# A transformer stack on one core: the two heads of a pair given to the scheduler ahead of the next pair's projections

## The chip, the cores and the metric

The kernel runs on one core of a Trainium2 chip. The metric is the device time of one execution, in microseconds, as the median of several runs. Three runs of the kernel before took 1758.92, 1760.01 and 1761.11 us; the median is 1760.01 us.

## The reference, cut to what matters

The input x has 512 positions of 1024 channels, in float32. Four attention layers come first: MLA, sliding window (SWA), forget-gate attention (FOX), MLA. A second block follows (four mixers, a SwiGLU feed-forward, a gated embedding), which the change doesn't touch. Each of the four layers has 16 heads, and its shape is the same:

```python
h = x @ w_in                                   # queries, keys, values, gate (MLA: through low ranks)
s = q @ k.T * scale (+ per-head bias), causal   # per head; SWA: a window of 128 keys
o = softmax(s) @ v                              # per head, 512 x 64
y = (o * silu(gate)) @ w_out
x = layernorm(8 ** 0.25 * x + y)
```

## The kernel before, in words

**Precision.** Every large product is made from high and low parts in fp32r: `mm3` (L155 to L159) issues three matmuls for one product of 128 contraction rows. A weight block is loaded by SyncE (`w`, L135), its high part is cast on ScalarE (L138) and its low part is subtracted on GpSimd (L139).

**One attention layer.** Heads go two by two, as eight pairs. `pairs` (L586) is the loop over them, and MLA, SWA and FOX hand it three things:

- `prep(p)`: the projections of pair p. They write the `acc` banks of PSUM, and ScalarE and VectorE copy them out into high and low tiles. SWA: one query projection of 24 matmuls of 512 columns, and for pairs 0 and 4 a key projection (L655). FOX: a query and a key projection of 24 matmuls each (L723), for every second pair the values of the group, and for each head a bias tile (a DMA of a row broadcast, and four additions on GpSimd, L737 and L738). MLA: small projections from the low ranks, for every second pair values of the group, and three kinds of DMA that place parts of queries and keys (L520, L187).
- `head(d, p, e)`: `attend` (L390). Scores on TensorE into the two `s` banks, the bias and the row maximum on VectorE (L403), exponentials on ScalarE (L419), the division on VectorE (L427), transposes on TensorE into the two `t` banks (L443), the split of the transposed block on ScalarE and VectorE (L184, L185), and the product with the values into the one `o` bank (L452). The scores of a head live in a tile `p`, of which there are two. In these layers a head issues no DMA and nothing on GpSimd.
- `gate(p)` (L601): a projection of 24 matmuls of 512 columns, tanh on ScalarE (L605) and one operation on VectorE (L606).

`join` (L458) copies a head's output out of the `o` bank (L462 on ScalarE, L463 on VectorE) and `gated` (L465) multiplies with the gate. The output projection (`out_proj`, L283, through `layer_end`) follows: 192 matmuls of 512 columns, of which 21 of every chain of 24 don't need the last pair.

**What sets the order.** The kernel does not write out the order of an engine's queue. The program is given to the framework's scheduler (L1133), which plays it through with its own estimates of time and so lays down the order of each engine's instructions and which buffer each tile gets. Instructions that depend on one another keep their order; among those that are ready, the place in the given program ranks them. An instruction that is not ready is passed over, so a later piece of the program can run earlier. On the chip each queue is then fixed.

In the loop of `pairs` the given order is: the projections of pair p+1 (L593), the two heads of pair p (L594 and L595), the gate of pair p (L597), the gating (L598). FOX takes the pairs in the order 6, 7, 0, 1, 2, 3, 4, 5 (L749), the others from 0 to 7.

Of the kernel before, what the change touches and what calls it, by code (L numbers as in the profile page):

```python
# [88 lines left out]
class Kern:  # L89
# [496 lines left out]
    def pairs(s, order, prep, head, Wg, g0, xT, oT):  # L586

        order = list(order)
        u = {order[0]: s.gate(order[0], Wg, g0, xT)}
        d = prep(order[0])  # L590
        for p, after in zip(order, order[1:] + [None]):
            og = s.t("f", [P, S], name="og")
            nd = prep(after) if after is not None else None  # L593
            for e in range(2):  # L594
                s.join(og, e, head(d, p, e))  # L595
            if p not in u:
                u[p] = s.gate(p, Wg, g0, xT)  # L597
            s.gated(p, og, u[p], oT, after is None)  # L598
            d = nd
# [537 lines left out]
```

## Time and profile before

| | |
|---|---|
| runs shown | 1758.92, 1760.01, 1761.11 us; median 1760.01 us |
| profiled execution, its own time | 1762.84 us |
| span of the profiled execution | 1761.1 us |
| mean granted TensorE clock | 0.979 |
| busy: PE, PEld, VectorE, ScalarE, GpSimd | 96%, 81%, 55%, 50%, 49% |
| the pair loops in the span | MLA about 72 to 257 us, SWA 308 to 480, FOX 547 to 783, MLA 868 to 1046 |

TensorE is busy nearly everywhere, so the share of busy time alone doesn't show where time can be won. The table of stretches is read with two columns together: the busy time of TensorE against the length of the stretch, and the granted clock.

### The profile page before, as it was taken

The page shows a single profiled execution, that of the slowest core. Times are in us where ns is not written, and L with a number is a line of the kernel's source. Part 1 is how long each engine was busy: PE and PEld are TensorE (multiplying, and loading weights), DVE is VectorE, ACT ScalarE, POOL GpSimd, SP SyncE. Part 2 cuts the span into 40 slices and gives each one's busy share as a digit, 9 for nine tenths or more (in the row PEclk, how much of TensorE's full clock was granted, in tenths as well). Part 3 has the DMA queues.
Part 4 walks back from the last instruction along what each step waited for, and adds up shares of the span by engine and source line. Part 5 has one row for each costly group of instructions (what it writes and reads, how often), then busy time and mean ns, then how long its engine had stood idle before and what let it go on. Part 6 is the DMA issues. An engine that isn't in the chain of part 4 may idle for free.

```text
span 1761.1 us, 25691 instructions
## 1 busy us (share of the span) xinstructions
PE 1684.8 (96%) x8818; PEld 1435.2 (81%) x8818; DVE 962.0 (55%) x2223; ACT 873.8 (50%) x2054; POOL 854.4 (49%) x775
## 2 busy tenths in 40 slices
PE   8999999999999999999999998999999999999999
PEld 7888878887788888778888877877778888888877
DVE  4587654677654665766587665599544222210053
ACT  4576543666445655633576642755544333332351
POOL 1644534444255665616644523745644444443571
PEclk9999999999999999999999998999999999999999
DMA  5434534322032333314444523332332333332332
GB/s 169 132 98 114 165 104 124 99 70 87 26 97 81 101 88 93 116 51 127 120 110 103 176 61 74 91 81 64 114 90 83 98 96 96 96 100 80 105 99 72
DMA packets 190339, 173.91 MB, mean 99 GB/s; under 512 B 14280, under 2 KB 154952, under 8 KB 190208
## 3 DMA queue, kind: packets, MB, share of 16 engines
q1 hardware_dynamic: 190208, 172.27, 33.9%
q8 instruction: 70, 1.15, 0.3%
q14 instruction: 61, 0.50, 0.1%
HBM read 150.94 MB, written 6.87 MB: 90 GB/s over the span
## 4 chain that ended last, share of the span: by engine, by line
PE 52%; DVE 9%; ACT 2%; issue 2%; POOL 2%; DMA 1%; SPq 0%; ACTq 0%; POOLq 0%; DVEq 0%
PE ps_acc L157 11%; PE ps_acc L158 11%; PE ps_acc L159 11%; PE ps_s L158 4%; PE ps_s L157 4%; PE ps_s L159 4%; PE ps_o L452 2%; PE ps_t L443 2%; DVE p L427 1%; DVE sel L926 1%; ACT p L419 1%; DVE m L925 1%; DVE p L403 1%; PE ps_s L238 1%; DVE ptl L185 1%
## 5 line engine op out<-in xcount | busy, mean ns | idle before, releaser
L139 POOL TENSOR_TENSOR wl<-wr,wh 128x512 fp32r<-128x512 f32 (+2 forms) x362 | 472.7, 1316 | 421.5 <-ACT wh L138 408.7
L138 ACT CAST wh<-wr 128x512 fp32r<-128x512 f32 (+2 forms) x368 | 223.6, 613 | 364.9 <-PE ps_acc L158 125.1
L157 PE MATMUL ps_acc<-act,wh 128*128 128x512 f32 (+1 forms) x880 | 331.5, 377 | 0.9 <-DVE v L620 0.8
L158 PE MATMUL ps_acc<-act,wh 128*128 128x512 f32 (+1 forms) x880 | 330.2, 375 | 0.3 <-DVE act L185 0.2
L159 PE MATMUL ps_acc<-act,wl 128*128 128x512 f32 (+1 forms) x880 | 330.1, 375 | 0.0
L157 PEld LDWEIGHTS ps_acc<-act,wh 128*128 128x128 f32 x880 | 165.6, 188 | 27.9 <-PE ps_acc L159 1.2
L159 PEld LDWEIGHTS ps_acc<-act,wl 128*128 128x128 f32 x880 | 165.3, 188 | 27.5
L158 PEld LDWEIGHTS ps_acc<-act,wh 128*128 128x128 f32 x880 | 165.4, 188 | 27.0 <-DVE act L185 0.7
L419 ACT ACTIVATE p<-p,st 128x256 f32<-128x256 f32 (+3 forms) x288 | 153.5, 537 | 32.8 <-DVE st L410 17.3
L157 PE MATMUL ps_acc<-wh,act 128*128 128x256 f32 (+3 forms) x384 | 134.5, 350 | 7.7 <-ACT act L469 3.1
L185 DVE TENSOR_TENSOR ptl<-ps_t,pth 128x512 fp32r<-128x512 f32 (+1 forms) x200 | 117.6, 597 | 38.5 <-ACT pth L184 37.7
L184 ACT CAST pth<-ps_t 128x512 fp32r<-128x512 f32 (+1 forms) x200 | 100.3, 516 | 72.5 <-PE ps_t L443 63.0
L443 PE MATMUL ps_t<-c_ident,p 128*128 128x128 f32 x672 | 116.9, 283 | 17.3 <-DVE p L427 12.4
L427 DVE TENSOR_SCALAR p<-p,st 128x256 f32<-128x256 f32 (+3 forms) x264 | 132.1, 559 | 1.8
L159 PE MATMUL ps_acc<-wh,act 128*128 128x256 f32 (+3 forms) x384 | 130.7, 341 | 0.1
L158 PE MATMUL ps_acc<-wl,act 128*128 128x256 f32 (+3 forms) x384 | 130.4, 340 | 0.0
L443 PEld LDWEIGHTS ps_t<-c_ident,p 128*128 128x128 f32 x672 | 82.0, 143 | 33.7 <-DVE p L427 13.2
L452 PE MATMUL ps_o<-pth,v 128*128 128x256 f32 (+3 forms) x288 | 90.1, 318 | 6.3 <-DVE og L463 4.4
L452 PE MATMUL ps_o<-ptl,v 128*128 128x256 f32 (+3 forms) x288 | 88.2, 335 | 4.3 <-DVE ptl L185 4.2
L157 PEld LDWEIGHTS ps_acc<-wh,act 128*128 128x128 f32 x384 | 77.8, 203 | 16.0 <-ACT act L469 3.3
L158 PEld LDWEIGHTS ps_acc<-wl,act 128*128 128x128 f32 x384 | 77.7, 202 | 5.1 <-issue 0.5
L159 PEld LDWEIGHTS ps_acc<-wh,act 128*128 128x128 f32 x384 | 77.1, 201 | 5.5 <-DVE act L185 0.3
(371 smaller groups left out, 3801.3 us busy)
## 6 DMA issues: line engine op xcount, KB each, us to landing
wr<-in_w_gate_up_dram SPq DMA_DIRECT2D x88, 256.0 KB, 2.8
wr<-in_fox_w_in_dram SPq DMA_DIRECT2D x60, 256.0 KB, 3.1
wr<-in_w_in_dram SPq DMA_DIRECT2D x48, 256.0 KB, 2.9
wr<-in_w_down_dram SPq DMA_DIRECT2D x44, 256.0 KB, 2.6
wr<-in_swa_w_in_dram SPq DMA_DIRECT2D x40, 256.0 KB, 2.9
wr<-in_mla_w_in_dram SPq DMA_DIRECT2D x32, 256.0 KB, 3.1
qk<-qk SPq DMA_DIRECT2D x32, 256.0 KB, 3.1
wr<-in_mla_w_out_dram SPq DMA_DIRECT2D x32, 256.0 KB, 3.5
```

The lines of the kernel that those rows point to most:

```text
L138: nc.scalar.copy(h, raw)
L139: (nc.vector if dve else nc.gpsimd).tensor_sub(l, raw, h.bitcast(F32))
L157: mm(out, lh, rh, start=first, stop=False)
L158: mm(out, lh, rl, start=False, stop=False)
L159: return mm(out, ll, rh, start=False, stop=last)
L184: s.nc.scalar.copy(hi, src)
L185: s.nc.vector.tensor_sub(lo, src, hi.bitcast(F32))
L238: mm(out, q[:, e, c], kd[:, kk], start=True, stop=False)
L419: nc.scalar.activation(a, a, AF.Exp, bias=st[:, 1, i:i + 1], scale=scale, accum_out=st[:, 2, i:i + 1])
L427: nc.vector.tensor_scalar_mul(a, a, st[:, 3, i:i + 1])
L443: nc.tensor.transpose(ps[:, n:n + P], sc[:, c:c + P], s.ident)
L452: nc.tensor.matmul(o[:, j * P:j * P + m], vj, pp[:, c:c + m], start=first, stop=k == 1 and grp[-1] == max(2, grp[-1]) and j == grp[-1], sk ...
```

## The change

The call of `prep` for the next pair moves from ahead of the two heads to behind them. What is computed stays the same, and no instruction is added or removed.

```diff
         for p, after in zip(order, order[1:] + [None]):
             og = s.t("f", [P, S], name="og")
-            nd = prep(after) if after is not None else None
             for e in range(2):
                 s.join(og, e, head(d, p, e))
+            nd = prep(after) if after is not None else None
             if p not in u:
                 u[p] = s.gate(p, Wg, g0, xT)
             s.gated(p, og, u[p], oT, after is None)
```

## Rows read from the trace of the kernel before

**Rows 1.** The page's first part: the span, and busy time, share of the span and instructions of each engine.

```profile
span 1761.1 us, 25691 instructions
PE 1684.8 (96%) x8818; PEld 1435.2 (81%) x8818; DVE 962.0 (55%) x2223; ACT 873.8 (50%) x2054; POOL 854.4 (49%) x775
```

**Rows 2.** Busy time by stretch: the stretch, its length, then busy time and count of PE, PEld, DVE, ACT, POOL, the granted clock, the DMA share, GB/s. Each pair loop is cut in its body and its end; the last row is a stretch of the feed-forward.

```profile
72.00:204.00 132.00, 129.07 (x717) 111.02 (x717) 94.87 (x271) 86.04 (x238) 61.15 (x59) 0.99 0.48 129
204.00:257.00 53.00, 46.46 (x224) 37.66 (x223) 34.18 (x77) 28.16 (x64) 24.30 (x19) 0.94 0.40 124
308.00:428.00 120.00, 115.29 (x620) 98.18 (x619) 87.64 (x244) 78.99 (x203) 52.81 (x41) 0.99 0.28 84
428.00:480.00 52.00, 46.54 (x226) 37.69 (x225) 36.15 (x93) 27.36 (x73) 13.57 (x12) 0.90 0.14 44
547.00:742.00 195.00, 191.36 (x1082) 167.02 (x1081) 121.74 (x310) 118.35 (x282) 113.25 (x116) 0.98 0.34 95
742.00:783.00 41.00, 35.73 (x167) 29.07 (x167) 27.20 (x60) 21.57 (x53) 14.24 (x12) 0.92 0.23 67
868.00:1001.00 133.00, 129.01 (x723) 110.44 (x721) 99.12 (x278) 87.29 (x240) 62.66 (x59) 1.00 0.48 131
1001.00:1046.00 45.00, 41.86 (x209) 34.73 (x209) 26.02 (x67) 23.22 (x55) 12.08 (x9) 0.96 0.28 86
1408.00:1452.00 44.00, 44.00 (x195) 36.44 (x195) 9.44 (x12) 14.43 (x24) 21.18 (x17) 1.00 0.34 99
```

**Rows 3.** The timeline of PE at the end of FOX's loop: start, length, engine, line, tiles. The first row is the last matmul of the last gate, the second the first of the output projection.

```profile
741.83 0.39 PE L159 MATMUL ps_acc<-act,wl 128*128 128x512 f32 x1
742.06 0.39 PE L157 MATMUL ps_acc<-wh,act 128*128 128x512 f32 x1
```

**Rows 4.** The timeline of VectorE from 742 to 778 us, its joins alone: one row ends one head of FOX.

```profile
751.72 0.68 DVE L463 TENSOR_TENSOR og<-ps_o,og 64x512 f32<-64x512 f32 x1
760.82 0.69 DVE L463 TENSOR_TENSOR og<-ps_o,og 64x512 f32<-64x512 f32 x1
769.32 0.68 DVE L463 TENSOR_TENSOR og<-ps_o,og 64x512 f32<-64x512 f32 x1 [0.47 <-ACT og L462]
776.24 0.69 DVE L463 TENSOR_TENSOR og<-ps_o,og 64x512 f32<-64x512 f32 x1
```

**Rows 5.** The group of PE's instructions from 742 to 783 us with the longest wait: busy time, mean ns of one, then the idle time before them and what ended it.

```profile
L157 PE MATMUL ps_acc<-wh,act 128*128 128x512 f32 x12 | 5.1, 421 | 3.1 <-ACT act L469 3.1
```

**Rows 6.** The timeline of PE around the scores of the first head of FOX's pair 3: the two matmuls of one score block (L238, L239), and the rows next to them.

```profile
690.15 0.22 PE L238 MATMUL ps_s<-qk 128*128 128x128 f32 x1
690.21 0.46 PE L157 MATMUL ps_acc<-act,wh 128*128 128x512 f32 x1
...
703.07 0.39 PE L159 MATMUL ps_acc<-act,wl 128*128 128x512 f32 x1
703.30 0.22 PE L239 MATMUL ps_s<-kl,qk 128*128 128x128 f32 x1
```

**Rows 7.** The groups of PE instructions between those two, from 690.25 to 703.28 us: the projections among them.

```profile
L157 PE MATMUL ps_acc<-act,wh 128*128 128x512 f32 x16 | 6.4, 401 | 0.0
L158 PE MATMUL ps_acc<-act,wh 128*128 128x512 f32 x16 | 6.4, 399 | 0.0
L159 PE MATMUL ps_acc<-act,wl 128*128 128x512 f32 x16 | 6.3, 392 | 0.0
```

**Rows 8.** The timeline of VectorE: the last copy of a pair's projections out of PSUM (L185, L204, L228), and L403, the first operation of a head on its scores. In order of time: MLA pair 3's first head, MLA pair 4's key, MLA pair 4's first head; SWA pair 7's query, SWA pair 6's first head, SWA pair 7's first head; FOX pair 1's key and first head; FOX pair 3's first head, its block after the wait of rows 6, FOX pair 4's key and first head.

```profile
122.24 0.68 DVE L403 CUSTOM_DVE_ANT_0 p<-ps_s,c_mask 128x512 f32<-128x512 f32 x1
...
134.04 0.68 DVE L185 TENSOR_TENSOR qk<-ps_acc,qk 128x512 fp32r<-128x512 f32 x1
...
146.84 0.68 DVE L403 CUSTOM_DVE_ANT_0 p<-ps_s,c_mask 128x512 f32<-128x512 f32 x1
...
421.08 0.69 DVE L204 TENSOR_TENSOR qk<-ps_acc,qk 64x512 fp32r<-64x512 f32 x1
...
426.77 0.28 DVE L403 CUSTOM_DVE_ANT_0 p<-ps_s,win 128x128 f32<-128x128 f32 x1
...
447.35 0.28 DVE L403 CUSTOM_DVE_ANT_0 p<-ps_s,win 128x128 f32<-128x128 f32 x1
...
616.50 0.69 DVE L228 TENSOR_TENSOR kl<-ps_acc,qk 64x512 fp32r<-64x512 f32 x1
...
625.05 0.68 DVE L403 CUSTOM_DVE_ANT_0 p<-ps_s,rope 128x512 f32<-128x512 f32 x1
...
686.86 0.68 DVE L403 CUSTOM_DVE_ANT_0 p<-ps_s,rope 128x512 f32<-128x512 f32 x1
...
703.56 0.29 DVE L403 CUSTOM_DVE_ANT_0 p<-ps_s,b 128x128 f32<-128x128 f32 x1 [3.89 <-PE ps_s L239]
...
710.01 0.69 DVE L228 TENSOR_TENSOR kl<-ps_acc,qk 64x512 fp32r<-64x512 f32 x1
...
724.48 0.69 DVE L403 CUSTOM_DVE_ANT_0 p<-ps_s,rope 128x512 f32<-128x512 f32 x1 [0.95 <-issue]
```

**Rows 9.** The timeline of PE: the scores of FOX pair 3's first head, and the last transposes of the head two before it.

```profile
681.80 0.40 PE L239 MATMUL ps_s<-kl,qk 128*128 128x512 f32 x1
...
686.65 0.62 PE L443 MATMUL ps_t<-c_ident,p 128*128 128x128 f32 x4
```

**Rows 10.** The waits of SyncE's queue, the longest: who waited for whom, us in total, times, the longest.

```profile
SPq L135 <- POOL wl L139: 755.1, 309, 19.7
```

## The prediction

> **What bounds the kernel now.** I read the page first: TensorE is busy 96% of a span of 1761.1 us, the next engine, VectorE, 55% [rows 1]. The kernel is bound by TensorE, so a change of order can only win back time in which TensorE stands idle or runs at a lower granted clock, or lose more of it. Next I cut the span by stage. A stretch of the feed-forward shows what full speed is: 44.00 of 44.00 us busy, clock 1.00, 195 matmuls of 512 columns, that is 0.2256 us for each [rows 2]. Against that stand the four pair loops. I add, for each stretch, the idle time of PE and the time lost to the clock (one minus the granted clock, times the length). The ends of the loops lose 6.5 + 3.2 = 9.7 us (first MLA, 204 to 257), 5.5 + 5.2 = 10.7 (SWA, 428 to 480), 5.3 + 3.3 = 8.6 (FOX, 742 to 783) and 3.1 + 1.8 = 4.9 (second MLA, 1001 to 1046), 33.9 us together; the bodies lose 4.2, 5.9, 7.5 and 4.0 us [rows 2]. The rest of the kernel isn't touched. So 34 us at the ends are the most that I look for, and the question is what makes them.
>
> The timeline answers it for FOX. The last gate's last matmul starts at 741.83 us and the output projection at 742.06 [rows 3], but four heads end after that, at 751.72, 760.82, 769.32 and 776.24 plus 0.69 us [rows 4]: 8.2 us from one to the next. Projections have run ahead and heads have fallen behind, so at the end there is little for TensorE besides the chains of single heads. Is it the order of this change that holds the heads back? The score block of 128 columns of FOX pair 3's first head says yes: its first matmul starts at 690.15, its second, which needs only tiles that an earlier block of the same head had used at 681.80, at 703.30 [rows 6, 9]. Between them lie 48 matmuls of 512 columns [rows 7]. That is twice 24, the query and the key of the next pair in FOX's order, pair 4: its key is copied out at 710.01 [rows 8]. VectorE stood idle 3.89 us for that second matmul [rows 8]. In the given order those 48 stand ahead of these heads; the change puts them behind.
>
> **The change part by part.** Nothing is added or removed; `prep` of the next pair loses its rank over the two heads. It changes the order only where both are ready at once.
>
> *FOX.* There they are: pair 3's heads begin at 686.86 and pair 4's key is copied out at 710.01 [rows 8]. What goes: a wait of up to 13.15 us in one head (703.30 minus 690.15) [rows 6]. What is late next: the head's tile `p`. The first operation of pair 3's first head, on scores ready after 681.80, runs at 686.86, right behind the last transposes of the head two before it, at 686.65 [rows 8, 9]; so part of any gain is spent waiting for one of two tiles. I take that heads come out one spacing, 8.2 us, earlier relative to the projections, less than the 13.15. A head's own TensorE work is 6400 columns (2560 of scores, 1280 of transposes, 2560 of the product), at 0.2256 us for 512 columns 2.8 us. Today's end, from 742 to the last join at 776.9, is 34.9 us long and has 4 x 2.8 + 19.0 = 30.2 us to fill it (19.0: four chains of 21 matmuls of the output projection that don't need the last pair); 4.7 us remain, near the 5.3 idle [rows 2]. With three heads left it is 26.7 us against 8.4 + 19.0 = 27.4: no gap. But the last join, its gating and casts are then still awaited, and the wait for them is 3.1 us [rows 5]. So of 8.6 us I count 8.6 - 3.1 = 5.5 as won. Bounds: 8.6 above; below see the second rival.
>
> *MLA, twice.* Mostly the next projections are finished long before the pair begins, but where a group's values are due they overlap: pair 3's heads begin at 122.24, pair 4's key is copied out at 134.04 [rows 8]. The body loses 4.2 and 4.0 us in all, and this is one of two such places in each [rows 2]. Between 0 and 4 I take 0.75 each, near the lower end, because a TensorE that stalls there is also short of projections, which now come later.
>
> *SWA.* Pair 7's query is copied out at 421.08, before pair 6's first head begins at 426.77 [rows 8]. Where the projections are through before the heads are ready, rank decides nothing: 0, upper bound the 10.7 us of its end.
>
> *The queues moved past.* Every DMA of `prep` (weights, FOX's rows, MLA's placing, SWA's window) sits in SyncE's queue, and FOX's bias additions in GpSimd's. A head puts nothing in either, so the order within both queues stays except against the gate's, which it already preceded and still does. SyncE mostly waits for free weight tiles (755.1 us) [rows 10]; a projection that runs later frees them later. I cost that at nothing, covered by the distance from copy-out to need: 14.5 us for FOX's pair 4 (724.48 minus 710.01), 12.8 for MLA's pair 4 (146.84 minus 134.04), 26.3 for SWA's pair 7 (447.35 minus 421.08), and least, 8.6, for FOX's pair 1 (625.05 minus 616.50) [rows 8]. Two heads of FOX put 5.6 us of TensorE work ahead of the projections, less than each of these.
>
> *Interleaving.* More changes between projections and small matmuls of heads come in. The most finely mixed stretch, the second MLA's body, runs at a clock of 1.00; the clock falls at the ends, where PE waits (0.90 and 0.92) [rows 2]. So I cost the mixing at nothing. [...]
>
> *Sum.* 5.5 + 2 x 0.75 = 7.0 us. Against the profiled execution's own 1762.84 us that is 1755.8. The median of the runs is 2.8 us below that execution, so for the median I say 1760.0 - 7.0 = **1753.0 us**.
>
> **The rivals.**
>
> *No change.* The heads are slow because only two `p` tiles exist, not because of rank. For it: rows 9, and SWA, whose end loses most though its projections run more than a pair ahead [rows 2, 8]. Against it: the 13.15 us of rows 6. Then the time is 1760, give or take the reshuffle of a few places, within 3.5. [...]
>
> *Slower: the next pair starves.* If the scheduler pushes `prep` not by 5.6 us of TensorE work but behind both heads' whole chains, 2 x 8.2 = 16.4 us, the distances above are used up: by 7.8 us at FOX's pair 1, 1.9 at its pair 4, 3.6 at MLA's pair 4. Heads would start late, and what they lose appears at the loop's end, where nothing covers it. With FOX's 7.8 alone it gives 1768; with MLA's twice, 1775. It decides from the point where the copy-out of `prep` comes more than 8.6 us later against its pair. For it: MLA's and FOX's distances are short. Against it: TensorE has gaps in every chain, and whatever is ready fills them.
>
> *All ends close.* If the lag of heads goes in all four loops, up to 33.9 us are won: 1726. Against it: SWA's 421.08 and 426.77.
>
> **How the numbers follow.** A measurement of this kernel can tell about 0.2%, 3.5 us, from no change. My forecast (3.5 to 14 us faster): 0.42. More than 14 faster: 0.08. No change: 0.28. Slower: 0.22. So faster 0.50, same 0.28, slower 0.22. The order is laid down anew for four loops, and rows show only some of the places that move, so the range goes to 1738 (two thirds of the large case's way) and to 1768 (the second rival's first price); I leave out 0.07 below and 0.10 above. The likeliest case alone spans 1746 to 1756.5.
>
> **What would show it.** Right: in FOX no head's score block split by 48 matmuls, three heads or fewer ending after the last gate, PE busier and the clock above 0.92 at that end; SWA's end much as before. Wrong: distances from copy-out to first operation of a head below zero slack with PE idle in a loop's body; or the same four heads left over at an unchanged end. The prediction as a whole fails if loops that I cost at nothing, SWA above all, move by more than FOX does.

## The result and the profile after

The change makes the kernel slower: 1781.2 us (median of 1786.51, 1782.02, 1778.68 and 1780.39) against 1759.5 us in the same session, ratio 1.013, 95% interval 1.0102 to 1.0157, or 18 to 28 us lost. The forecast was 1753.0 us, its range ended at 1768. The profiled execution after took 1786.51 us of its own, the longest of these four.

The page's engine line of the kernel after, in answer to [rows 1]:

```profile
span 1784.7 us, 25695 instructions
PE 1701.3 (95%) x8818; PEld 1443.8 (81%) x8818; DVE 963.3 (54%) x2223; ACT 878.7 (49%) x2054; POOL 852.7 (48%) x775
```

The work is the same, 8818 matmuls. To see in which layer the time went, take the end of the last transpose of each layer's output (L248) as a milestone, in both profiles; between two milestones lies one layer:

| layer | before, us | after, us | difference |
|---|---|---|---|
| load of x | 13.9 | 15.2 | +1.3 |
| MLA | 273.7 | 282.7 | +9.1 |
| SWA | 224.6 | 226.9 | +2.3 |
| FOX | 308.4 | 301.6 | -6.7 |
| MLA, second | 263.9 | 281.8 | +17.9 |
| all behind | 676.6 | 676.4 | -0.2 |

FOX gained 6.7 us in this profile, where 5.5 was forecast. The two MLA layers, forecast at 0.75 us of gain each, lost 27. The busy time by stretch of the kernel after, in the columns of [rows 2] (MLA's body and end, FOX's, the second MLA's):

```profile
72.00:204.00 132.00, 122.62 (x649) 103.93 (x648) 90.03 (x262) 83.16 (x226) 55.14 (x54) 0.95 0.41 106
204.00:268.00 64.00, 59.96 (x295) 48.99 (x294) 38.47 (x89) 32.85 (x76) 30.34 (x24) 0.97 0.50 150
555.00:747.00 192.00, 191.04 (x1102) 167.39 (x1101) 126.24 (x315) 120.66 (x290) 117.08 (x120) 1.00 0.35 98
747.00:789.00 42.00, 37.00 (x167) 29.81 (x166) 25.73 (x55) 20.23 (x46) 14.80 (x11) 0.88 0.28 80
873.00:1005.00 132.00, 121.50 (x628) 102.02 (x627) 89.37 (x260) 80.07 (x220) 52.08 (x52) 0.92 0.37 94
1005.00:1070.00 65.00, 62.33 (x311) 50.43 (x308) 38.92 (x87) 32.48 (x76) 23.79 (x18) 1.00 0.48 139
```

Add idle time of PE and time lost to the clock, as the prediction did. MLA's body loses 9.4 + 6.6 = 16.0 us where it lost 4.2, the second MLA's body 10.5 + 10.6 = 21.1 where it lost 4.0. Their ends lose less than before (6.0 and 2.7 against 9.7 and 4.9). FOX's body loses 1.0 in place of 7.5.

So the question is what holds up PE in MLA's body. The forecast had looked at pair 4's key copied out to its first head [rows 8]; here is that pair after, on VectorE:

```profile
146.97 0.68 DVE L185 TENSOR_TENSOR qk<-ps_acc,qk 128x512 fp32r<-128x512 f32 x1
...
156.90 0.69 DVE L403 CUSTOM_DVE_ANT_0 p<-ps_s,c_mask 128x512 f32<-128x512 f32 x1 [2.39 <-PE ps_s L159]
```

The copy-out came 12.9 us later than before (134.04), the head 10.1 us later (146.84). Who waits? SyncE's own queue, from 100 to 225 us, has one wait that the kernel before does not have in its list; columns: engine and line, what it waited for, total us, times, longest:

```profile
SPq L477 <- POOL qr L762: 18.3, 2, 14.1
```

and its timeline shows the hole of 17 us between two DMAs that place queries:

```profile
124.61 0.50 SPq L477 DMA_DIRECT2D qk<-qk  x1
141.64 1.15 SPq L477 DMA_DIRECT2D qk<-qr  x2
```

`qr` L762 is the last step of `rope` (L752), the rotation of the next group's queries. Its two steps on VectorE, L757 and L758, one right behind the other (134.12 and 134.73 us after), empty the acc bank that its matmuls wrote. Timelines of PE (last matmul of that projection), ScalarE (first copy of a join, L462; a gate's tanh, L605) and VectorE (L757), first of the kernel before:

```profile
98.27 0.39 PE L159 MATMUL ps_acc<-cq,wl 128*128 128x512 f32 x1
...
110.84 0.58 ACT L462 COPY og<-ps_o 64x512 f32<-64x512 f32 x1 [0.34 <-PE ps_o L452]
111.45 0.60 ACT L605 ACTIVATE f<-ps_acc 128x512 f32<-128x512 f32 x1
...
111.55 0.69 DVE L757 TENSOR_TENSOR f<-ps_acc,cos 128x512 f32<-128x512 f32 x1
```

and then of the kernel after:

```profile
104.17 0.39 PE L159 MATMUL ps_acc<-cq,wl 128*128 128x512 f32 x1
...
116.89 0.58 ACT L462 COPY og<-ps_o 64x512 f32<-64x512 f32 x1 [0.41 <-PE ps_o L452]
117.50 0.60 ACT L605 ACTIVATE f<-ps_acc 128x512 f32<-128x512 f32 x1
...
134.12 0.68 DVE L757 TENSOR_TENSOR f<-ps_acc,cos 128x512 f32<-128x512 f32 x1
...
135.85 0.58 ACT L462 COPY og<-ps_o 64x512 f32<-64x512 f32 x1
136.46 0.60 ACT L605 ACTIVATE f<-ps_acc 128x512 f32<-128x512 f32 x1
```

Before, the rotation runs 12.9 us behind its matmuls, beside the first join of pair 1. After, it runs 29.6 us behind them, beside the first join of pair 2. All that time it holds one of three acc banks. VectorE is 68% busy in this body, so it was free to run the rotation long before.

**The theory** (the rope theory below, after the name of the rotation's routine). The rotation needs two tiles named `f`, of which there are four. So does each pair: its output `og`, first written by its first join, and its gate's `u`. If the slots of one tile name are given out in the order in which the program first writes its tiles, the line before is og1, u1, a, b, og2, u2 (a and b are the rotation's); the change makes it og1, u1, og2, a, b, u2. The rotation then has to wait for a join one pair later, whatever is free. The calls that make these tiles come in the same order in both kernels (og2, a, b, u2); only the order of first writes differs. It fits that the tanh of each gate stands behind the first join of its pair: by 0.6 us for pairs 1 to 7 of the first MLA before, by 0.6 to 3.2 us after. It fits too that the layer's three rotations after start at 95.81, 134.12 and 178.88 us, close to the first joins of pairs 0, 2 and 4 (97.19, 135.85 and 181.18), behind which they are now placed. The line is laid down when the scheduler plays the program through; on the chip the rotation can start a little ahead of the join, on another engine, here by 1.4 to 2.3 us. The rival theory (the values theory below) is that the values and projections come late because heads now rank ahead of them.

What PE idles for, from 873 to 1005 us of the kernel after, is spread over many small waits:

```profile
PE ps_o L452 <- DVE ptl L185: 2.8, 3, 2.2
PE ps_s L157 <- DMA qk<-kr: 2.1, 2, 1.9
```

The second, 0.2 us before, falls at 883.54 us, ahead of SyncE's first wait for `qr` in this layer (a hole from 927 to 942 us), so it isn't an effect of such a hole. No long wait of PE in this stretch names SyncE's late placing: how the late rotation turns into pauses of PE isn't traced here.

### The profile page after: what moved, and what is told of

The parts are those of the page before. It is cut to its first block, busy times and chain, and to the rows that moved or that the text cites. A ratio compares the mean times of both kernels' runs of the same rounds, so it can differ in the third digit from the quotient of the medians.

```text
span 1784.7 us, 25695 instructions
## 1 busy us (share of the span) xinstructions
PE 1701.3 (95%) x8818; PEld 1443.8 (81%) x8818; DVE 963.3 (54%) x2223; ACT 878.7 (49%) x2054; POOL 852.7 (48%) x775
## 4 chain that ended last, share of the span: by engine, by line
PE 62%; DVE 11%; POOL 3%; ACT 3%; issue 3%; DMA 2%; SPq 0%; POOLq 0%; ACTq 0%; DVEq 0%
PE ps_acc L157 13%; PE ps_acc L158 13%; PE ps_acc L159 13%; PE ps_s L157 4%; PE ps_s L158 4%; PE ps_s L159 4%; PE ps_o L452 3%; PE ps_t L443 2%; DVE p L427 2%; ACT p L419 1%; DVE p L403 1%; POOL wl L139 1%; DVE sel L926 1%; PE ps_s L238 1%; DVE ptl L185 1%
## 5 line engine op out<-in xcount | busy, mean ns | idle before, releaser
L419 ACT ACTIVATE p<-p,st 128x256 f32<-128x256 f32 (+3 forms) x288 | 153.5, 535 | 35.0 <-DVE st L410 15.2
L185 DVE TENSOR_TENSOR ptl<-ps_t,pth 128x512 fp32r<-128x512 f32 (+1 forms) x200 | 118.0, 598 | 52.1 <-ACT pth L184 51.1
L157 PE MATMUL ps_acc<-wh,act 128*128 128x256 f32 (+3 forms) x384 | 132.0, 344 | 6.7 <-ACT act L469 3.1
L159 PE MATMUL ps_acc<-wh,act 128*128 128x256 f32 (+3 forms) x384 | 129.3, 338 | 0.1
L443 PEld LDWEIGHTS ps_t<-c_ident,p 128*128 128x128 f32 x672 | 83.3, 145 | 29.4 <-DVE p L427 11.8
```

Of the source, the lines that this page charges most:

```text
L157: mm(out, lh, rh, start=first, stop=False)
L159: return mm(out, ll, rh, start=False, stop=last)
L185: s.nc.vector.tensor_sub(lo, src, hi.bitcast(F32))
L419: nc.scalar.activation(a, a, AF.Exp, bias=st[:, 1, i:i + 1], scale=scale, accum_out=st[:, 2, i:i + 1])
L443: nc.tensor.transpose(ps[:, n:n + P], sc[:, c:c + P], s.ident)
```

## The experiments

Each ran in five rounds against the kernel before; times are medians, ratios those to the kernel before with their 95% intervals.

| run | us | ratio | interval |
|---|---|---|---|
| fox_alone | 1754.7 | 0.9967 | 0.9951 to 0.9984 |
| mla_odd | 1779.2 | 1.0106 | 1.0079 to 1.0132 |
| mla_even | 1768.6 | 1.0038 | 1.0023 to 1.0052 |
| after_rope | 1776.4 | 1.0081 | 1.0058 to 1.0105 |
| q_late | 1777.4 | 1.0099 | 1.0081 to 1.0118 |
| q_late_rope | 1775.9 | 1.0086 | 1.0069 to 1.0103 |
| odd_rope | 1773.5 | 1.0078 | 1.0056 to 1.0099 |
| before_rope | 1771.8 | 1.0063 | 1.0042 to 1.0085 |
| q_late_claim | 1761.0 | 0.9996 | 0.9983 to 1.0009 |
| after_claim | 1754.8 | 0.9951 | 0.9933 to 0.9969 |
| swa_alone | 1760.1 | 0.9984 | 0.9972 to 0.9996 |
| fox_gate_claim | 1756.3 | 0.9961 | 0.9945 to 0.9977 |
| mla_claim | 1769.7 | 1.0055 | 1.0039 to 1.0071 |
| odd_claim | 1761.3 | 1.0008 | 0.9993 to 1.0022 |

Several of these kernels are the same order of instructions, measured more than once. Compared row by row on every engine (by operation, tile names and shape; of SyncE the DMAs; the added writes of the claims left out):

- swa_alone is the kernel before;
- q_late is mla_odd;
- q_late_rope and odd_rope are both before_rope;
- mla_claim is mla_even;
- q_late_claim is the kernel before, but for one DMA of SyncE (SWA's window) two places later.

Within such a group the ratios differ by up to 0.0023 (before_rope and q_late_rope), so a difference of that size between two runs of the table is no finding.

**By layer and by pair: fox_alone, mla_odd, mla_even, swa_alone.** `pairs` gets a rule that says for which pairs prep goes behind the heads.

```diff
-            nd = prep(after) if after is not None else None
+            behind = late(after)
+            nd = prep(after) if after is not None and not behind else None
             for e in range(2):
                 s.join(og, e, head(d, p, e))
+            if behind:
+                nd = prep(after)
```

fox_alone: 

> FOX alone gets the new order, MLA and SWA keep the old one. By the layer times of the two profiles (FOX 308.4 us before, 301.6 after) this should give 6.7 us: 1753 us (1750 to 1756), all theories. If FOX's gain in the changed kernel came only from what the layers ahead of it had left behind, the time stays within 3 us of the kernel before.

mla_odd: 

> Only in the two MLA layers, and only for the pairs 1, 3, 5, 7, prep goes behind the heads; these preps carry the query projection and rotation of the next group. Rope theory (the rotation of the next group's queries gets its two f tiles only behind the output tile of the pair that it is now placed behind, and SyncE's queue and an acc bank wait for it): nearly the whole MLA loss of 9.1 + 17.9 = 27 us, so 1779 to 1787 us. Values theory (the values and projections of a group's first pair, now ranked behind the heads, come too late): at most 5 us of loss, 1758 to 1765.

mla_even: 

> Only in the two MLA layers, and only for the pairs 2, 4, 6, prep goes behind the heads; these preps carry the values of their group. Rope theory: 1757 to 1765 us, the rotation keeps its place. Values theory: most of the 27 us of loss, 1779 to 1787.

swa_alone: 

> The new order in SWA alone. Forecast on record: nothing, since the projections there are through before the heads; the profile of the changed kernel has SWA 2.3 us longer. So 1759 to 1764, ratio 1.000 to 1.002.

FOX alone wins 5.8 us (0.0033 of 1760; interval 2.8 to 8.6), near the 5.5 forecast. That is not far above the 0.0023 of the groups, but the layer itself bears it out: by the milestones FOX takes 298.2 to 301.6 us in the five profiles with its new order and 305.3 to 309.5 in the eleven with the old one. Its body and end, in the columns of [rows 2]:

```profile
537.00:733.00 196.00, 193.90 (x1112) 169.32 (x1111) 129.98 (x313) 120.99 (x291) 119.72 (x124) 1.00 0.35 96
733.00:774.00 41.00, 36.88 (x173) 29.62 (x172) 25.87 (x57) 21.33 (x49) 14.39 (x11) 0.93 0.28 86
```

The body loses 2.1 us where it lost 7.5, the end 4.1 + 2.9 = 7.0 where it lost 8.6. The odd pairs, whose prep carries the next group's queries, lose 18.7 us, the even ones 6.7: together 25.4, near the 27 of the two layers. The odd pairs came out where the rope theory had them; the even ones lie between the ranges of the two theories, so something else costs there. In swa_alone the scheduler lays down the same order as before on every engine, instruction for instruction. Its ratio of 0.9984 is therefore no gain.

**The one step: q_late.** From the kernel before, only the call of `queries` moves.

```diff
             kt = s.split_heads(ps, lambda e: kr)
-            if pr and g < 3:
-                G["q", g + 1] = queries(g + 1)
...
             for e in range(2):
                 s.join(og, e, head(d, p, e))
+            if behind is not None:
+                behind(after)        # queries(g + 1) for odd pairs
```

> The kernel before, except that in the two MLA layers the projection and rotation of the next group's queries alone go behind the two heads; every other projection keeps its old place. Rope theory in its strong form (this one step carries the loss of the odd pairs): most of the 18.7 us that the odd pairs' whole prep cost, 1774 to 1782. Rival (the queries and keys of the pair itself are what comes late): 1758 to 1766.

It loses 17.4 us, nearly all that mla_odd lost (18.7), in mla_odd's order of instructions. So the odd pairs' own queries and keys don't matter: moving them as well changes nothing. VectorE's and ScalarE's timelines show the rotation once more beside the first join of pair 2:

```profile
132.92 0.68 DVE L761 TENSOR_TENSOR f<-ps_acc,cos 128x512 f32<-128x512 f32 x1
...
134.65 0.58 ACT L462 COPY og<-ps_o 64x512 f32<-64x512 f32 x1
```

**Without f tiles: after_rope, q_late_rope, odd_rope, before_rope.**

```diff
-        a = s.t("f", [P, S])
-        b = s.t("f", [P, S])
+        a, b = lo.bitcast(F32), hi.bitcast(F32)
```

after_rope: 

> The changed kernel, whole, with the rotation's two intermediate f tiles replaced by the two halves of its own output tile qr (same operations, same places in the program). Rope theory: the rotation no longer stands in the line for f tiles, so it runs soon after its matmuls, the wait of SyncE for qr (14.1 us at its longest) goes, and most of the 27 us of MLA comes back: 1754 to 1762 us. Values theory: 1776 to 1784, as the changed kernel.

q_late_rope: 

> As q_late, with the rotation worked in the two halves of its output tile, so that it takes no f tiles. Rope theory: what q_late loses against the kernel before comes back but for 3 us. If being late by rank alone is the cause, it stays at the time of q_late, within 3 us.

odd_rope: 

> Prep of MLA's odd pairs behind the heads, as in mla_odd, with the rotation worked in its output tile. Rope theory: 1758 to 1766, near the kernel before. If only a third of the loss hangs on the line for f tiles, as after_rope (1.0081 against 1.0130) suggests: 1769 to 1774.

before_rope: 

> The control: the kernel before with the rotation worked in its output tile, the order of the program as it was. The rotation is not late there (it starts 13 us after its matmuls), so both theories say within 4 us of the kernel before; if the line for f tiles costs something in the old order too, some us faster.

By their times all four missed what was expected. after_rope came out in the range of the values theory, q_late_rope stayed at the time of q_late, odd_rope lies where only a third of the loss would hang on the f tiles, and the control before_rope, expected within 4 us of the kernel before, lost 11 us (0.0063). In q_late_rope the rotation starts at 109.51 us, 23 us earlier than in q_late at the same place in the program, so its lateness did come from the f tiles:

```profile
102.04 0.40 PE L159 MATMUL ps_acc<-cq,wl 128*128 128x512 f32 x1
...
109.51 0.69 DVE L760 TENSOR_TENSOR qr<-ps_acc,cos 128x512 f32<-128x512 f32 x1 [1.30 <-issue]
```

The control says why these times can't be read against the kernel before: the program's order is the old one there. There is one `qr` tile, and the rotation's first step now waits for it: from 66 to 200 us VectorE stands idle ahead of that step for DMAs that read the tile (`qk<-qr`), 1.9 us once in the control and 5.0 us in two waits in q_late_rope. In the control's MLA, from 72 to 204 us, PE waits for the bank that the rotation's second step (L757 there) empties:

```profile
PE ps_acc L157 <- DVE qr L757: 2.6, 1, 2.6
```

One wait was exchanged for another; what else makes up the control's 11 us is open. But the order laid down decides what the times leave open. q_late_rope and odd_rope are the control, instruction for instruction. Once the rotation takes no f tile, the place of the odd pairs' prep behind the heads changes nothing: rank by itself has no part in what q_late and mla_odd lose. after_rope holds the even pairs and FOX as well, so its 1.0081 says nothing on this.

**The line itself: q_late_claim, after_claim, odd_claim, mla_claim.** Nothing is moved back; GpSimd writes one column of a and b at the old place in the program, six tiles in each MLA layer. That makes it the first write of these tiles.

```diff
+        def claim(p):
+            if p is not None and p % 2 and p < 7:
+                ab = [s.t("f", [P, S]) for _ in range(2)]
+                for t in ab:
+                    nc.gpsimd.memset(t[:, :1], 0.0)
+                G["ab", p // 2 + 1] = ab
...
+            if claim is not None:
+                claim(after)
             for e in range(2):
                 s.join(og, e, head(d, p, e))
```

q_late_claim: 

> As q_late (rotation of MLA's next queries behind the two heads), but GpSimd writes one column of its two f tiles at the old place in the program, ahead of the heads; no tile is added. Line theory (the slots of a tile name are handed out in the order in which the program first writes its tiles): the rotation starts again about 13 us after its matmuls, and the time is that of the kernel before, 1757 to 1764. If the rank of the matmuls and of the rotation is the cause, it stays at q_late's 1775 to 1779.

after_claim: 

> The changed kernel, whole, with the same one column of the rotation's two f tiles written ahead of the heads. Line theory: its 1.0130 less the 0.0099 of q_late, 1.003 or so, 1764 us, and lower if the even pairs' loss comes from the same line: down to 1755. If the line is not the cause: 1778 to 1785.

odd_claim: 

> The new order in MLA's odd pairs alone, with the same claim. If the line was all that the odd pairs paid: 0.998 to 1.002, 1758 to 1765 us. If the odd pairs' rank wins what the even pairs' loses: 0.994 to 0.997, 1751 to 1757. If part of mla_odd's 0.0106 is rank: 1.003 and more.

mla_claim: 

> The new order in the two MLA layers alone, for all pairs, with one column of the rotation's f tiles written ahead of the heads. From the other runs: after_claim 0.9951 over fox_alone 0.9967 and swa_alone 0.9984 leaves 1.000, so 1758 to 1764 us. If the even pairs' rank costs its 0.0038 here too: 1767 to 1771.

q_late goes from 1.0099 to 0.9996, and mla_odd from 1.0106 to 1.0008. The rotation's place in the program, and that of its matmuls, is still behind the heads, and yet the order laid down is the old one. What moved it was the line alone. The timelines of GpSimd, PE and VectorE in q_late_claim: the claim at 110.33, and the rotation where it was in the kernel before.

```profile
97.44 0.39 PE L159 MATMUL ps_acc<-cq,wl 128*128 128x512 f32 x1
...
110.33 0.14 POOL L550 MEMSET f<- 128x1 f32 x2
...
110.72 0.69 DVE L769 TENSOR_TENSOR f<-ps_acc,cos 128x512 f32<-128x512 f32 x1
```

The whole change with the claim, after_claim, falls from 1.0130 to 0.9951: 31 us for twelve small writes, and faster than both kernels, by 8.6 us against the kernel before (5.5 to 11.8). The forecast's 7.0 us are there once the line is kept, but all in FOX: in its profile the MLA layers take 273.3 and 266.5 us (273.7 and 263.9 before), FOX 298.2.

mla_claim came out at 1.0055, in the second of the two ranges expected. It is mla_even's order over again: with the claim the odd pairs add nothing, and the even pairs' rank costs 6.7 to 9.7 us by itself when FOX has the old order. By the milestones it is all in the second MLA (mla_even +9.8 us, mla_claim +6.4), none in the first (-1.6 and +0.2). PE waits there for a join (first row) and for the score bank; waits of PE in mla_claim from 957 to 982 us (in the same stretch before, the first is 0.3 us and the second is not there):

```profile
PE ps_o L452 <- DVE og L463: 2.2, 2, 1.7
PE ps_s L157 <- DVE st L403: 1.6, 2, 0.8
```

The second MLA of after_claim, laid down behind another FOX, loses 2.5 us and not 6.4 against the profile before; against that of fox_alone (259.8 us, in the fastest of its runs) it loses 6.7, so single profiles don't settle it. By the single parts after_claim should have stood at 0.9967 x 1.0055 = 1.0022, not at 0.9951, a gap of 0.0071. Why the even pairs' cost doesn't show there is open.

**A second place where the line shows: fox_gate_claim.** Here FOX has the new order, and in all three kinds of layer one column of the gate's `u` is written ahead of `og`'s first write.

```diff
+            if p not in u:
+                t = s.t("f", [P, S])
+                s.nc.gpsimd.memset(t[:, :1], 0.0)
             og = s.t("f", [P, S], name="og")
```

> The new order in FOX alone, as in fox_alone (0.9967), and in all three kinds of layer one column of the gate's f tile is written ahead of the pair's output tile. Line theory: the gate's tanh no longer stands behind the first join of its pair and gives its acc bank back earlier; the tanh then starts soon after the gate's matmuls in the profile. What that is worth is open: an acc bank free for some 15 us of each pair could win 3 to 10 us over fox_alone, or nothing where f tiles run short for it.

In fox_alone the tanh of pair 1's gate follows the first join as in the kernel before; matmul and ScalarE rows:

```profile
93.36 0.39 PE L159 MATMUL ps_acc<-act,wl 128*128 128x512 f32 x1
...
111.08 0.58 ACT L462 COPY og<-ps_o 64x512 f32<-64x512 f32 x1 [0.34 <-PE ps_o L452]
111.68 0.60 ACT L608 ACTIVATE f<-ps_acc 128x512 f32<-128x512 f32 x1
```

With the claim it runs 15 us ahead of that join:

```profile
91.69 0.40 PE L159 MATMUL ps_acc<-act,wl 128*128 128x512 f32 x1
...
97.01 0.58 ACT L612 ACTIVATE f<-ps_acc 128x512 f32<-128x512 f32 x1
...
112.01 0.59 ACT L462 COPY og<-ps_o 64x512 f32<-64x512 f32 x1
```

So the line holds for the gate's tile as well. The bank freed earlier wins nothing here: 0.9961 against fox_alone's 0.9967.

## Why the prediction was wrong, step by step

- **FOX: right in sum, half right in place, and the sum partly by luck.** The score block that was split by 13.15 us [rows 6] is whole: no FOX block of the kernel after has its two matmuls more than 2 us apart. Three heads end after the last gate, not four [rows 3, 4], though barely: a fourth head's join starts at 753.44 us, 0.3 us ahead of the gate's last matmul. That matmul is the first row below, then the joins of VectorE.

```profile
753.72 0.63 PE L159 MATMUL ps_acc<-act,wl 128*128 128x512 f32 x1
...
765.55 0.68 DVE L463 TENSOR_TENSOR og<-ps_o,og 64x512 f32<-64x512 f32 x1
...
774.86 0.68 DVE L463 TENSOR_TENSOR og<-ps_o,og 64x512 f32<-64x512 f32 x1 [0.48 <-ACT og L462]
...
781.72 0.68 DVE L463 TENSOR_TENSOR og<-ps_o,og 64x512 f32<-64x512 f32 x1
```

  Yet the end is no fuller (5.0 + 5.0 = 10.0 us lost, clock 0.88, where above 0.92 was forecast); the gain came in the body (1.0 us lost in place of 7.5), for which the sum counted nothing. That a sum made at the end came near what the body won is luck.
- **The step that failed** is "It changes the order only where both are ready at once". The place in the program also decides in which order tiles of one name are given out. So a block that is ready may have to wait for an earlier-placed tile that nobody needs yet. From that sentence followed the 0.75 us of gain for each MLA layer, with bounds of 0 and 4 and no loss: the queries of the next group counted as one more projection, passed by two heads (5.6 us by FOX's). q_late and q_late_claim show that moving this one block cost 17 us, and the runs without f tiles that rank by itself moved nothing in the odd pairs: taken as a sentence on rank it held there.
- **MLA's even pairs** were in the same term. They cost 6.7 to 9.7 us by themselves, and that is rank: their prep takes no f tile and shares no other tile name with the heads and joins that pass it. What in the second MLA makes it so stays open.
- **The queues.** "I cost that at nothing" left out that SyncE would stand 14.1 us for the late rotation, with keys (placed at 142.88 us) and weights (149.45) of the next pairs behind it. That this stand is what costs isn't shown. The fastest kernel, after_claim, has one as long in its first MLA (90 to 215 us), for a copy-out:

```profile
SPq L477 <- DVE qk L185: 20.1, 4, 14.7
```

  How the loss divides between SyncE's queue, the acc bank held 29.6 us and the order that the scheduler made around them wasn't separated by any run.
- **SWA: right**, 0: the order laid down is the same.
- **Interleaving and the clock.** The mixing shows no cost: in FOX's body PE changes 206 times between matmuls into acc banks and others, 151 times before, and its clock is 1.00 (0.98 before). By this count the prediction's "most finely mixed stretch", the second MLA's body with 96 changes in 133 us before, was no finer mixed than FOX's, 151 in 195. In the second MLA after, cut in stretches of 15 us, the lowest clock stands where PE paused most; that stretch and its neighbours:

```profile
920.00:935.00 15.00, 14.04 (x78) 11.50 (x76) 13.46 (x43) 9.39 (x27) 3.03 (x3) 0.93 0.30 71
935.00:950.00 15.00, 11.86 (x58) 10.24 (x57) 12.46 (x37) 10.07 (x31) 3.91 (x3) 0.73 0.12 27
950.00:965.00 15.00, 15.00 (x77) 12.71 (x76) 6.96 (x14) 9.43 (x21) 11.04 (x13) 1.00 0.59 149
```

  With 3.1 us of pauses, 2.2 of them in one piece up to 944.56 us, the granted clock is 0.73, and the five matmuls of 512 columns from 946.97 to 948.67 us start 0.43 us apart. In the next stretch, with no pause, it is 1.00, and from 950.29 to 952.60 us they start 0.23 us apart. Clock and pauses don't match in every stretch: from 980 to 995 us 2.7 us of pauses stand beside 0.98, from 995 to 1010 us none beside 0.91. That the pauses lowered the clock wasn't shown by a run of its own. In this body the clock took as much as the pauses, 10.6 against 10.5 us; in the first MLA's body it took 6.6 against 9.4. In FOX's body PE's idle time fell from 3.6 to 1.0 us as the clock rose from 0.98 to 1.00.
- **The rivals.** "The next pair starves" had the outcome right for MLA, late heads, and a price of 1775 against 1781. Its own sign did not come: pair 4's copy-out came 12.9 us later, but against its pair only 2.9 us (from 12.8 to 9.9 us ahead of the head), not 8.6. Nor did its cause, so the nearness of its price is luck: the scheduler did not push prep behind whole chains, and FOX's pair 1, its first place, did not starve (its first operation came at 627.6 us, against 625.05 before, in a loop that began 8.4 us later). "No change" had the better hunch in naming tiles, though of another name (`f`, not `p`), and not their number: after_claim has no tile more. (Its row for the `p` tile [rows 9] was read one head too late: 686.65 is the first transpose of the head one before; the last of the head two before start at 686.08. They too lie just ahead of 686.86, so the reading stands.) "All ends close" did not come.
- **The range** ended at 1768 because only FOX's slack was used for the loss; MLA's second price, 1775, was left outside.

## What to carry to other kernels

Before moving a block in a program that a scheduler lays out, list the tile names that it shares with what it passes, and write down the order of first writes before and after. If a short-lived tile falls behind a long-lived one of the same name, claim it early: the rank can move, the line should not. A name of its own would take it out of the line too, but no run here has one; working the rotation in its output tile instead brought a wait of its own (before_rope, 1.0063). The sign to look for is an instruction that runs long after its inputs are ready while its engine had time. And before reading a difference between two variants, compare the orders laid down: two variants can come out as one and the same.

## What was not expected

- Twelve writes of one column (0.09 to 0.14 us each on GpSimd) were worth 31 us.
- A gate's tanh stands in that line too, 18 us behind its matmuls in the kernel before (93.36 plus 0.39 to 111.68 in fox_alone, whose first MLA layer is laid down as there); freeing it won nothing.
- Kernels with the same order of instructions differ by up to 0.0023 in the ratio, and by up to 4.5 us in one layer of a single profile (MLA of fox_alone, 269.2 against 273.7), so a layer's difference of that size in one profile is no finding.
